# Issuing a transformer trunk's late stores from GpSimd's queue instead of SyncE's

## The chip, the core and the metric

The program runs on one NeuronCore of a Trainium2 chip. The core has a matmul engine (TensorE, "PE" in the profile; its weight loads are shown apart as "PEld"), a vector engine (VectorE, "DVE"), an engine for activation functions and copies (ScalarE, "ACT"), GpSimd ("POOL") and SyncE ("SP"), which computes nothing and here issues transfers. Each engine works through its own list of instructions in order; where an instruction needs a result of another engine or a transfer, it waits, and everything behind it on that engine waits too. Data moves between the chip's large memory (DRAM in the program) and the on-chip memory (SBUF) by DMA. A DMA is put in a queue by an engine's instruction and carried out by sixteen DMA engines; the profile names the queue fed by SP "hardware_dynamic" and the one fed by GpSimd "software_dynamic".

The metric is the device time of one execution in microseconds (us), as the median of several runs.

## The reference

Two streams of 512 tokens of width 1024 ("prompt", stream 0, and "sample", stream 1) go through the same two layers with the same weights, all in float32.

```python
def _trunk(x, ...):
    for i in range(DEPTH):                       # 2 layers
        xn = _rms_norm(x, pre_norm_g[i])
        if i % N_MIXERS == 0:
            h = _rwkv7_branch(xn, ...)           # layer 0: a scan over tokens, both directions
        else:
            h = _natten_branch(xn, ...)          # layer 1: neighbourhood attention
        x = x + _rms_norm(h, post_norm_g[i])
    return x

def _wkv7_scan(r, decay, k, v, a, b, reverse):   # layer 0, 16 heads of 64
    def step(s, inp):
        r_t, w_t, k_t, v_t, a_t, b_t = inp
        sa = jnp.einsum('bhvk,bhk->bhv', s, a_t)
        s = s * w_t[:, :, None, :] + sa[..., None] * b_t[:, :, None, :] + v_t[..., None] * k_t[:, :, None, :]
        return s, jnp.einsum('bhvk,bhk->bhv', s, r_t)
...
def _natten_branch(xn, w_in, b_in, rpb, w_o, b_o):
    proj = xn @ w_in + b_in                      # 1024 -> 4 x 1024
    q, k, v, z = jnp.split(proj, 4, axis=-1)
    o = _neighbourhood_attention(heads(q) * (HEAD_DIM ** -0.5), heads(k), heads(v), rpb)
    return (o.reshape(bsz, t, D_INNER) * jax.nn.silu(z)) @ w_o + b_o
```

Layer 0 also has projections r, k, v, z and an output projection `w_o`. In layer 1 each of the 512 tokens (a grid of 8 x 64) attends to an 8 x 16 window, with a learned bias per head.

## The kernel before

Activations lie transposed: 128 features on the partitions, 512 tokens along the row, so a 512 x 1024 matrix is eight tiles of 128 x 512 floats (256 KB each). One column of a projection is a sum over eight such tiles, and each float32 product is made of three matmuls (`gemm`, lines 428 to 430: high part of the weight by high and low part of the data, low part by high part). Weights come from DRAM as `raw` tiles (three buffers), and ACT (line 377) and DVE (line 378) split them into `whi` and `wlo`.

The program has three stages. First both streams are normalized and some projections made. Then the scan stage (`scan_phase`) runs the scans of both streams and, woven into them by an order written out by hand with an estimated clock, the projections of stream 1 and the beginning of layer 1 for stream 0. What follows is `rest`, the stage behind the scan, from about 1169 us on: the last two columns of stream 0's q, k, v, z (`inproj(0, ...)`), the output projection of stream 1's layer 0 (`out0(1)`), the attention of stream 0 (`heads(0, p)`, eight pairs of heads), its output projection and result (`out1(0)`), the projections of stream 1 in layer 1 (`inproj(1, ...)`) with the attention of stream 1 woven in (`heads(1, p)`), and `last`, which makes stream 1's output by tokens. `rest` is not ordered by hand: a scheduler that estimates times places the instructions of each engine, so a moved store also moves what stands around it.

A projected column doesn't go straight to its reader: `qkvz` computes the tile `o` (a `tmp` buffer of five) from PSUM (the matmul engine's output memory) on DVE (line 1393) and ACT (lines 1397 to 1407), and `save` (line 327) stores it to DRAM as `dq`, `dk`, `dv` or `dz`. `heads` later loads it back (`load`, line 333) as `q`, `k`, `v`, `z`, into buffers of its own; the load waits until the store has landed. From q and k PE makes scores (`sc`, line 1437), DVE adds the bias and takes the maximum (line 1448), ACT takes exponentials (line 1451), DVE scales (line 1453), PE transposes (`pt`, line 1455), ACT copies (`pts`, line 1458), PE multiplies by the values (`po`, line 1470), and DVE applies the gate z (line 1479).

Which queue a store goes to is decided in `store`, by the flag `away`:

```python
    def store(self, kind):
        return self.nc.gpsimd if self.away and kind not in ("y", "x1", "h") else self.nc.sync
```

`away` is set to True at the start of `scan_phase` (line 1646) and to False at the start of `rest` (line 1750). So within the scan stage most stores are issued by GpSimd, and in `rest` all by SP, whose list also holds all the loads: weights, biases, q, k, v, z and the residual tiles.

Of the kernel before, what the change touches and what calls it, by code (L numbers as in the profile page):

```python
# [19 lines left out]
P = 128  # L20
# [211 lines left out]
class Trunk:  # L232
# [1252 lines left out]
    def out1(self, s):  # L1485
        nc = self.nc
        x = self.os[s]
        acc = self.t("acc1", pool=self.ap)
        hs = []
        for p in range(NP):  # L1490
            ps = yield from self.gemm(self.weight(self.a["w_ao"][p]), x, self.OUT1[p % 4])
            h = self.t("oa", (P, T), NP, F32, self.ap)
            nc.scalar.activation(h, ps, AF.Identity, bias=self.vec("bo", p))
            self.sumsq(acc, h, p, nc.vector if p == NP - 1 else nc.vector)
            hs.append(h)
            yield
        yield from self.rstds(acc, lambda: self.mm)
        rstd = acc
        for k, h in enumerate(hs):
            x = self.load(self.t("xr", bufs=self.NXR), self.sp["x1", s, k])  # L1500
            one = nc.vector.scalar_tensor_tensor(h, h, self.vec("post1", k), rstd, op0=ALU.mult, op1=ALU.mult)
            self.behind(one, self.mq)
            (nc.vector if k % 2 else nc.vector).tensor_tensor(h, h, x, op=ALU.add)
            nc.sync.dma_start(self.a["y"][s][k * P:(k + 1) * P, :], h)
            yield

    def by_token(self):
# [211 lines left out]
    def run(self):  # L1719
        self.todo = [(s, pb) for s in range(2) for pb in range(4)]  # L1720
        self.made, self.hid, self.shift = set(), {}, {}
        self.did = Counter()
        self.xz, self.os = [], [[], []]
        self.spare = None
        self.away = False
        mid, prep, first = ExitStack(), ExitStack(), ExitStack()
        self.banks(mid, pf=1, pm=5 - self.SG - self.ZY, us=1)
        if self.SG:
            self.banks(mid, pg=self.SG)
        self.zs = ExitStack()  # L1730
        self.banks(self.zs, zy=self.ZY)
        self.gt = "zy"
        self.lp = self.pool(first, "right")
        a = self.prelude(0)
        for _ in range(self.FIRST):
            next(a)
        a = both(a, self.prelude(1))
        run(self.columns(0, "z", self.xz), (a, 1))
        run(self.columns(0, "k", self.shifted(0, 1)), (a, 1))
        run(a)  # L1740
        self.xr = self.shifted(0, 0)
        first.close()
        self.front = self.pool(mid, "right")
        self.pp = self.pool(prep, "right")
        self.AHEAD, self.AHEADW = self.SCAN_A, self.SCAN_W
        self.scan_phase(mid)
        self.rest(prep, mid)

    def rest(self, prep, mid):
        self.away = False  # L1750
        prep.close()
        mid.close()
        self.banks(self.stack, pg=self.PG, pt=self.PT, po=1, sc=1, pm=5 - self.PG - self.PT)
        self.gt = "pg"
        self.ap = self.pool(self.stack)
        queue = [self.heads(0, p) for p in range(self.NPA)]

        def attention():
            while True:
                if queue and next(queue[0], self) is self:  # L1760
                    queue.pop(0)
                    continue
                yield

        a = attention()
        for p in range(self.NPA, NP):
            run(self.inproj(0, self.xa, p), (a, self.POST0))
            queue.append(self.heads(0, p))
        run(self.out0(1), (a, self.POST))
        while queue:  # L1770
            next(a)
        o = self.out1(0)
        if self.HS:
            with self.tc.high_priority(self.HS):
                next(o)
        n = KT * NP
        for _ in self.norm0(1):
            for _ in range(min(n, 3)):
                next(o)
                n -= 1  # L1780
        for _ in range(n):
            next(o)
        x = self.x1
        xt = self.by_token()
        for p, cs in [(p, range(4)) for p in range(6)] + [(6, range(3)), (7, range(3)), (6, (3,)), (7, (3,))]:
            run(self.inproj(1, x, p, cs), (a, self.POST3), (o, self.POST2), (xt, self.POST4))
            if 0 in cs:
                queue.append(self.heads(1, p))
        run(o)
        while queue:  # L1790
            next(a)
        self.last()
# [125 lines left out]
```

## Time and profile before

| | us |
|---|---|
| median of 3 runs | 1663.77 (1659.5 to 1666.94) |
| the profiled execution's own time | 1661.37 |
| its span, first to last instruction | 1659.6 |
| PE busy in it | 1557.8 (94%) |
| DVE busy | 1226.3 (74%) |
| ACT busy | 984.7 (59%) |
| POOL busy | 145.4 (9%) |
| mean granted TensorE clock | 0.979 |

The profile is one execution recorded instruction by instruction. A row of its timeline gives the start, the duration, the engine (SPq is SP's issuing of DMAs), the line of the kernel, the operation, "out<-in" by the names of the tiles, how many rows were merged (x2), and in brackets the idle time just before on that engine and what ended it. A row of waits names the waiting engine and line, then the operation that it waited for, the total, how many times, and the longest. "DMA dk<-tmp" as a releaser is the landing of the transfer that stored `tmp` to `dk`. Matmuls overlap in the pipeline, so the step from one start to the next, rather than the duration, is what a matmul costs.

### The profile page before, as it was taken

The numbers are of one execution on the slowest core, as the hardware profiler recorded it, in microseconds if no ns is written. First come the engines' busy times: TensorE is split into PE (matmuls) and PEld (weight loads), VectorE is DVE, ScalarE is ACT, GpSimd is POOL, SyncE is SP. The second block draws the span as 40 slices with busy tenths as digits, with TensorE's granted clock in tenths as the row PEclk, the third lists the DMA queues.
The fourth block names the chain that finished last, engine by engine and source line by source line (L and its number), as shares of the span: only waits on it lengthen the run. The fifth ranks groups of instructions, "written<-read, shape, count | busy, mean of one in ns | idle before, by whom it ended". The sixth has DMA issues, their size and how long they took to land.

```text
span 1659.6 us, 46414 instructions
## 1 busy us (share of the span) xinstructions
PE 1557.8 (94%) x18826; PEld 1193.4 (72%) x18826; DVE 1226.3 (74%) x2725; ACT 984.7 (59%) x1979; POOL 145.4 (9%) x278
## 2 busy tenths in 40 slices
PE   7989888898989998999988999999999999999998
PEld 5867566776767776776766777777777788777776
DVE  8995669688789787897788897855676585754564
ACT  5443665766756677665575665454677665555562
POOL 0000113311101224010000011000000000000000
PEclk9989999999999999999987999999999999999999
DMA  6435678776676788675867675554864346655553
GB/s 212 160 126 173 206 243 280 221 244 214 228 255 225 222 260 247 219 255 173 253 220 228 196 253 165 182 189 129 289 219 156 102 153 229 214 159 172 165 159 108
DMA packets 179894, 336.27 MB, mean 203 GB/s; under 512 B 20928, under 2 KB 53824, under 8 KB 179680
## 3 DMA queue, kind: packets, MB, share of 16 engines
q1 hardware_dynamic: 160864, 268.28, 50.2%
q0 software_dynamic: 18816, 65.02, 11.9%
q8 instruction: 148, 2.42, 0.6%
q14 instruction: 66, 0.54, 0.1%
HBM read 227.71 MB, written 105.51 MB: 201 GB/s over the span
## 4 chain that ended last, share of the span: by engine, by line
PE 46%; DVE 7%; DMA 6%; ACT 5%; issue 3%; POOL 0%; SPq 0%; DVEq 0%; ACTq 0%; POOLq 0%
PE pg L428 6%; PE pg L429 5%; PE pg L430 5%; PE pm L811 4%; PE pm L812 3%; PE pm L813 3%; PE sc L1437 2%; PE pf L1099 2%; DMA dk<-tmp 2%; PE po L1470 2%; PE us L1218 1%; PE pt L1455 1%; PE zy L1171 1%; PE us L1198 1%; PE zy L1222 1%
## 5 line engine op out<-in xcount | busy, mean ns | idle before, releaser
L811 PE MATMUL pm<-act,whi 128*128 128x512 f32 x640 | 283.6, 443 | 11.9 <-ACT whi L730 5.0
L812 PE MATMUL pm<-act,whi 128*128 128x512 f32 x640 | 257.1, 402 | 10.6 <-DVE act L758 6.5
L813 PE MATMUL pm<-act,wlo 128*128 128x512 f32 x640 | 256.1, 400 | 6.0 <-DVE wlo L732 5.9
L811 PEld LDWEIGHTS pm<-act,whi 128*128 128x128 f32 x640 | 122.0, 191 | 55.3 <-issue 11.4
L377 ACT CAST whi<-raw 128x512 fp32r<-128x512 f32 x148 | 91.5, 618 | 114.0 <-PE pg L429 67.1
L428 PE MATMUL pg<-act,whi 128*128 128x512 f32 x384 | 157.9, 411 | 0.4 <-DVE tmp L1393 0.4
L430 PE MATMUL pg<-act,wlo 128*128 128x512 f32 x384 | 152.1, 396 | 0.0
L429 PE MATMUL pg<-act,whi 128*128 128x512 f32 x384 | 152.0, 396 | 0.0
L812 PEld LDWEIGHTS pm<-act,whi 128*128 128x128 f32 x640 | 122.5, 191 | 36.6 <-DVE act L758 15.8
L813 PEld LDWEIGHTS pm<-act,wlo 128*128 128x128 f32 x640 | 122.4, 191 | 36.2 <-DVE wlo L732 9.6
L378 DVE TENSOR_TENSOR wlo<-raw,whi 128x512 fp32r<-128x512 f32 x148 | 101.5, 687 | 54.6 <-ACT whi L377 52.6
L732 DVE TENSOR_TENSOR wlo<-raw,whi 128x512 fp32r<-128x512 f32 x160 | 109.0, 684 | 35.5 <-ACT whi L730 35.2
L730 ACT CAST whi<-raw 128x512 fp32r<-128x512 f32 x160 | 97.9, 618 | 44.6 <-PE pm L812 23.4
L428 PEld LDWEIGHTS pg<-act,whi 128*128 128x128 f32 x384 | 72.2, 188 | 15.8 <-issue 3.3
L430 PEld LDWEIGHTS pg<-act,wlo 128*128 128x128 f32 x384 | 72.2, 188 | 15.5 <-issue 0.7
L429 PEld LDWEIGHTS pg<-act,whi 128*128 128x128 f32 x384 | 72.4, 189 | 13.2 <-issue 1.5
L1003 DVE TENSOR_TENSOR etmp<-N 128x30 f32<-128x30 f32 (+14 forms) x240 | 78.6, 328 | 4.3
L1005 DVE TENSOR_TENSOR N<-etmp,N 128x30 f32<-128x30 f32 (+14 forms) x240 | 78.7, 328 | 4.0
L1448 DVE CUSTOM_DVE_ANT_0 sb<-sc,bias 128x256 f32<-128x256 f32 x128 | 49.3, 419 | 34.6 <-PE pt L1455 22.7
L1451 ACT ACTIVATE sb<-sb,mx 128x256 f32<-128x256 f32 x128 | 64.0, 503 | 8.6 <-DVE mx L1450 8.1
L1099 PE MATMUL pf<-cab 64*64 64x128 f32 (+1 forms) x2048 | 66.6, 266 | 0.8 <-issue 0.8
L1210 ACT COPY X<-us 64x256 f32<-64x256 f32 x128 | 46.9, 366 | 25.3 <-PE zy L1077 21.4
(401 smaller groups left out, 3603.0 us busy)
## 6 DMA issues: line engine op xcount, KB each, us to landing
dab<-ab POOLq DMA_DIRECT2D x32, 1024.0 KB, 7.0
cab<-dab SPq DMA_DIRECT2D x64, 512.0 KB
raw<-in_w_in_dram SPq DMA_DIRECT2D x128, 256.0 KB
bias<-in_rpb_dram SPq DMA_DIRECT2D x32, 384.0 KB
raw<-in_w_z_dram SPq DMA_DIRECT2D x32, 256.0 KB
raw<-in_w_k_dram SPq DMA_DIRECT2D x32, 256.0 KB
raw<-in_w_r_dram SPq DMA_DIRECT2D x32, 256.0 KB
k<-dk SPq DMA_DIRECT2D x32, 256.0 KB
```

Source lines behind the costliest of these rows:

```text
L377: self.nc.scalar.copy(hi, src)
L378: (eng or self.nc.vector).tensor_tensor(lo, src, hi.bitcast(F32), op=ALU.subtract)
L428: nc.tensor.matmul(ps, hi, x[k][0], start=(k == 0), stop=False)
L429: nc.tensor.matmul(ps, hi, x[k][1], start=False, stop=False)
L430: self.mm = nc.tensor.matmul(ps, lo, x[k][0], start=False, stop=(k == KT - 1))
L730: nc.scalar.copy(hi, raw[h])
L732: nc.vector.tensor_tensor(lo, raw.pop(h), hi.bitcast(F32), op=ALU.subtract)
L811: nc.tensor.matmul(ps, hi[:, at], xh, start=(k == 0), stop=False)
L812: nc.tensor.matmul(ps, hi[:, at], xl, start=False, stop=False)
L813: nc.tensor.matmul(ps, lo[:, at], xh, start=False, stop=(k == KT - 1))
L1005: vt.tensor_tensor(N[:, q + 1:, :q], tv, N[:, q + 1:, :q], op=ALU.add)
L1099: end = nc.tensor.matmul(st.f[half(a), h, 0, d, g] if st.last else st.f[half(a), h, :, d, g], ab[half(h), d, g, 2 * e[d] + 1 - a], rt if s ...
```

## The change

The line that sets `away` back to False at the start of `rest` is gone, so the stores that `save` makes there, other than those of kinds y, x1 and h, are issued by GpSimd: eight tiles q, k, v, z of stream 0 (two columns of each), 32 of stream 1, and eight `xt` tiles (rows of stream 1's layer-0 result on the way back to tokens). The eight result stores of stream 0 in `out1` are written out as GpSimd's too. That makes 56 stores of 256 KB. Stream 1's result rows, stored in `last`, stay on SP, as do all loads.

```diff
@@ out1
             self.behind(one, self.mq)
             (nc.vector if k % 2 else nc.vector).tensor_tensor(h, h, x, op=ALU.add)
-            nc.sync.dma_start(self.a["y"][s][k * P:(k + 1) * P, :], h)
+            nc.gpsimd.dma_start(self.a["y"][s][k * P:(k + 1) * P, :], h)
             yield
@@ rest
     def rest(self, prep, mid):
-        self.away = False
         prep.close()
         mid.close()
```

Up to the end of the scan stage the lists of all engines are the same. Behind it the scheduler orders them anew. Three places show how.

On SP, in stream 1's projections: the load of `k` for one pair of heads waits for the store of the same tile. Rows with + are new, rows with - are gone; `raw` are weights, `bias` the attention's bias.

```order
 L333 DMA raw_20409<-in_w_in_dram 128x512
-L327 DMA dq_3784_20175<-tmp_20172 128x512
+L333 DMA raw_20411<-in_w_in_dram 128x512
 L333 DMA q_3847_20431<-dq_3784_20175 128x512
-L333 DMA raw_20411<-in_w_in_dram 128x512
 L333 DMA bias_20739<-in_rpb_dram 128x768 x2
 L333 DMA raw_20497<-in_w_in_dram 128x512
-L327 DMA dk_3802_20257<-tmp_20254 128x512
 L333 DMA k_3848_20433<-dk_3802_20257 128x512
 L333 DMA raw_20499<-in_w_in_dram 128x512
```

The two stores leave the list; the loads that wait for them stay, and one weight load now stands ahead of the load of q.

On PE, at the scores that read this same `k` (`sc_20465`, four matmuls in the list), among the projection's matmuls:

```order
 L429 MATMUL pg_20370<-act_18625,whi_20366 128x512
 L430 MATMUL pg_20370<-act_18626,wlo_20367 128x512
-L1437 MATMUL sc_20465<-k_3848_20433,q_3847_20431 128x256
+L428 MATMUL pg_20370<-act_18645,whi_20366 128x512
 L1470 MATMUL po_20153<-pts_20338,vtok_20132 64x128 x4
 L1470 MATMUL po_20153<-pts_20305,vtok_20132 64x128 x4
-L1437 MATMUL sc_20465<-k_3848_20433,q_3847_20431 128x256 x3
-L428 MATMUL pg_20370<-act_18645,whi_20366 128x512
+L1437 MATMUL sc_20465<-k_3848_20433,q_3847_20431 128x256 x4
 L429 MATMUL pg_20370<-act_18644,whi_20366 128x512
```

The first of the four score matmuls moves back by one projection matmul and the whole run of `po`, so `k` is needed later. The same move is made for the other three score groups around which PE waits for `k` (`sc_19843`, `sc_20776`, `sc_21050`).

On PE, in stream 0's attention, early in `rest`: before, two groups of scores of one pair of heads stand close together.

```order
L1437 MATMUL sc_17325<-k_3067_17286,q_3066_17284 128x256 x4
L1455 MATMUL pt_17181<-cc,sb_17207 128x128
L1455 MATMUL pt_17224<-cc,sb_17225 128x128 x2
L1455 MATMUL pt_17224<-cc,sb_17240 128x128 x2
L430 MATMUL pg_17302<-act_12735,wlo_17299 128x512
L428 MATMUL pg_17302<-act_12913,whi_17298 128x512
L429 MATMUL pg_17302<-act_12912,whi_17298 128x512
L430 MATMUL pg_17302<-act_12913,wlo_17299 128x512
L1424 MATMUL pm_17584<-cc,v_3156_17578 128x128 x4
L1437 MATMUL sc_17470<-k_3067_17286,q_3066_17284 128x256 x4
L1470 MATMUL po_17094<-pts_17252,vtok_17058 64x128 x4
L1470 MATMUL po_17094<-pts_17219,vtok_17058 64x128 x4
```

After the change the rows ahead of the second group are these, and the first group stands 27 rows ahead of it instead of 9:

```order
L429 MATMUL pg_17302<-act_12602,whi_17298 128x512
L430 MATMUL pg_17302<-act_12603,wlo_17299 128x512
L1470 MATMUL po_17094<-pts_17252,vtok_17058 64x128 x4
L1470 MATMUL po_17094<-pts_17219,vtok_17058 64x128 x4
L1437 MATMUL sc_17470<-k_3067_17286,q_3066_17284 128x256 x4
L1455 MATMUL pt_17330<-cc,sb_17331 128x128 x2
L1455 MATMUL pt_17330<-cc,sb_17343 128x128 x2
```

The attention of this pair is spread over more projection matmuls. An earlier pair moves the other way: before, `sc_16935` stood behind a run of `po` as `sc_17470` does here now; after the change only these rows of PE lie between it and the group ahead of it.

```order
L1437 MATMUL sc_16844<-k_2952_16815,q_2951_16813 128x256 x4
L1455 MATMUL pt_16713<-cc,sb_16714 128x128 x2
L1455 MATMUL pt_16713<-cc,sb_16726 128x128 x2
L1455 MATMUL pt_16743<-cc,sb_16744 128x128 x2
L1424 MATMUL pm_17059<-cc,v_3010_17053 128x128 x4
L1455 MATMUL pt_16743<-cc,sb_16761 128x128 x2
L1437 MATMUL sc_16935<-k_2952_16815,q_2951_16813 128x256 x4
```

Here the two groups of scores have moved closer together.

## Prediction

> **What bounds the kernel now.** I read the page's busy times first, then busy time by stretches behind the scan, then the waits of PE and of SP's queue there, and last the timeline around the longest of these waits. The stretches (start and end in us, length, then busy us and instructions of PE, PEld, DVE, ACT, POOL, the granted clock, the DMA share, GB/s):
>
> ```profile
> 1169.00:1320.00 151.00, 147.66 (x957) 116.56 (x956) 101.31 (x393) 103.28 (x250) 0.00 (x0) 1.00 0.60 201
> 1320.00:1440.00 120.00, 118.08 (x629) 95.28 (x628) 81.55 (x198) 70.28 (x140) 0.00 (x0) 1.00 0.59 187
> 1440.00:1610.00 170.00, 167.95 (x939) 129.97 (x938) 98.51 (x323) 92.55 (x212) 0.00 (x0) 1.00 0.54 169
> 1610.00:1660.00 50.00, 41.91 (x207) 33.15 (x205) 24.25 (x49) 14.21 (x33) 0.00 (x0) 0.95 0.33 109
> ```
>
> All that changes lies in these 491 us. Up to 1610 us PE is busy for 433.7 of 441; the last 50 us end with a tail on other engines. POOL does nothing at all. So a transfer can win only what PE stands idle for, and PE's waits behind the scan are few (who waits, for whom, total us, times, longest):
>
> ```profile
> PE sc L1437 <- DMA k<-dk: 2.1, 4, 0.6
> PE sc L1437 <- DVE mx L1448: 1.5, 1, 1.5
> PE pm L470 <- DVE tmp L466: 1.1, 1, 1.1
> PE pg L428 <- ACT oa L1493: 0.8, 1, 0.8
> PE pt L1455 <- DVE sb L1453: 0.7, 1, 0.7
> PE po L1470 <- ACT pts L1458: 0.6, 2, 0.3
> PE pg L428 <- DVE tmp L1393: 0.4, 1, 0.4
> ```
>
> Together 7.2 us. The first row is the one that the stores touch directly. SP's queue, over the same stretch, waits much longer for stores to land, because the loads of q, k, v, z stand in it:
>
> ```profile
> SPq L333 <- DMA dk<-tmp: 32.7, 8, 6.8
> ...
> SPq L333 <- DMA dq<-tmp: 18.5, 8, 3.5
> SPq L333 <- DMA dz<-tmp: 17.3, 8, 2.8
> SPq L333 <- DMA dv<-tmp: 12.8, 6, 2.7
> ```
>
> Here 81 us of store landings look like the prize, but nearly all of them pass while PE works. The timeline at one pair of heads shows how much is left:
>
> ```profile
> 1494.20 0.90 SPq L333 DMA_DIRECT2D bias<-in_rpb_dram  x2
> 1495.21 0.36 SPq L333 DMA_DIRECT2D raw<-in_w_in_dram  x1
> 1495.67 0.38 SPq L327 DMA_DIRECT2D dk<-tmp  x1
> 1502.78 0.33 SPq L333 DMA_DIRECT2D k<-dk  x1
> ...
> 1505.39 0.70 PE L1437 MATMUL sc<-k,q 64*128 64x256 f32 x2 [0.48 <-DMA k<-dk]
> ```
>
> The store of k is issued at 1495.67 and its reader can be issued only at 1502.78, 7.11 us later; the load takes until 1505.39; and PE stands still for 0.48 us of these ten.
>
> **The change, part by part.**
>
> *The issuing.* SP loses 56 issues and POOL gains them. On SP one took 0.38 us above, so 21 us leave SP's list; on POOL a store of the same kind, in the scan stage, took 0.54, so POOL gets 30 us in 491 in which it has nothing to do:
>
> ```profile
> L327 POOL DMA_DIRECT2D dk<-tmp x14: 540/541/569, 358.4 to 1151.1; - x14
> ...
> DMA to landing us min/median/max: 2.3/3.5/8.2
> ```
>
> The issue is 0.16 us longer for each tile on its way. The stores to `dxt`, `dv` and the result rows cost nothing: no PE wait above has them as its cause. POOL now waits in its list for each tile in turn; behind a waiting store stand only other stores, and they stood in the same order behind each other on SP. What else moves past SP's 56 gaps are the weight loads, and no row of PE's waits names a weight.
>
> *The landing of k.* On SP's queue it took at most 7.11 us; on POOL's, beside a busier DMA system, 3.5 in the middle and 8.2 at worst. Two bias loads and a weight load go out just ahead of it on SP's queue, and a store in a queue of its own need not stand behind them. I take 3.5, which brings k 3.5 us earlier. By itself that ends the first row of PE's waits, and the new order does so a second time: ahead of the scores PE now has one projection matmul and a run of `po` (16 in the trace). What a projection matmul costs stands in the timeline:
>
> ```profile
> 1429.42 0.40 PE L430 MATMUL pg<-act,wlo 128*128 128x512 f32 x1
> 1429.65 0.38 PE L1455 MATMUL pt<-cc,sb 128*128 128x128 f32 x2
> 1429.79 0.47 PE L428 MATMUL pg<-act,whi 128*128 128x512 f32 x1
> ```
>
> What a run of `po` costs stands in the chain of waits (start, us, what):
>
> ```profile
> 1262.61 1.03 PE po L1470 x16
> ```
>
> The projection matmul takes 0.23 (from 1429.42 to the next start at 1429.65) and the run of `po` 1.03, so 1.26 us of work lie in front of a wait that was 0.6 at most. The term is -2.1 us; its ends are 0 and -2.1.
>
> *PE's work in the new order.* The matmuls are the same, but what their mixture costs changes. Two transposes put between projection matmuls delay the next by 0.14 (1429.65 to 1429.79); four in one run cost this:
>
> ```profile
> 1427.26 0.60 PE L1455 MATMUL pt<-cc,sb 128*128 128x128 f32 x4
> 1427.62 0.48 PE L430 MATMUL pg<-act,wlo 128*128 128x512 f32 x1
> ```
>
> That is 0.36, so breaking a run saves 0.08. Counted over the two lists of PE, transposes go over into a projection matmul at 79 places instead of 69: ten breaks, -0.8 us. Since runs of scores and values are broken and joined too, I give it the ends 0 and -1.6.
>
> *The stall around 1230 us.* This is the second row of PE's waits, with the fifth and the last:
>
> ```profile
> 1221.99 0.81 SPq L333 DMA_DIRECT2D bias<-in_rpb_dram  x2
> 1223.37 1.34 SPq L333 DMA_DIRECT2D xr<-dy  x2
> ...
> 1228.20 1.34 ACT L377 CAST act<-xr 128x512 fp32r<-128x512 f32 x2 [3.31 <-DMA xr<-dy]
> 1231.70 1.14 PE L1437 MATMUL sc<-k,q 64*128 64x256 f32 x8 [1.53 <-DVE mx L1448]
> 1234.54 1.13 PE L1455 MATMUL pt<-cc,sb 128*128 128x128 f32 x6 [0.68 <-DVE sb L1453]
> 1236.43 0.49 PE L428 MATMUL pg<-act,whi 128*128 128x512 f32 x1 [0.43 <-DVE tmp L1393]
> ```
>
> The loads of y come late behind a bias load that waits for its buffer; ACT stands 3.31 us, and after it PE three times, 2.64 us in all, each time for DVE. In the new list the scores that waited 1.53 (`sc_17470`) stand 27 rows behind the group before instead of 9, so their wait goes. The bias load stays where it blocks SP, so ACT's wait may stay and reach PE elsewhere. I take -1.5, nearest to the row that the order removes, with the ends 0 and -2.6.
>
> *A new wait.* `sc_16935` has moved close to the group ahead of it (12 transposes between, 12 times 0.07 to 0.09 by the two rows above, about 1 us), while DVE must first have read that group. No row of before shows so close a pair; the nearest is the 1.53 us at `sc_17470`, an estimate for the worst, and 0 for the best. DVE has no load to wait for here, so I take +0.5.
>
> *The end.* The last gate tile is the place where a slower store would hurt:
>
> ```profile
> 1615.04 0.34 SPq L327 DMA_DIRECT2D dz<-tmp  x1
> 1617.09 0.34 SPq L333 DMA_DIRECT2D z<-dz  x1
> ...
> 1619.96 0.69 DVE L1479 TENSOR_TENSOR tmp<-po,z 128x512 f32<-128x512 f32 x1 [2.58 <-DMA z<-dz]
> 1621.34 0.69 DVE L378 TENSOR_TENSOR os<-tmp,os 128x512 fp32r<-128x512 f32 x1 [0.69 <-ACT os L377]
> 1624.91 0.39 PE L1557 MATMUL pg<-act,os 128*128 128x512 f32 x1
> ```
>
> The store lands within 2.05 us, the product with z is ready at 1622.03 and PE takes it at 1624.91. A landing of 3.5 uses 1.5 of these 2.9 us: nothing, until POOL's landing passes 4.9.
>
> Sum: -2.1 - 0.8 - 1.5 + 0.5 = -3.9 us, with ends of -6.3 and +1.5. The profiled execution took 1661.37 (1.77 more than its span), so 1657.5 for its like; the median of the runs shown is 2.4 above it, 1663.77, and becomes 1659.9.
>
> **What the skill says against it.** POOL's issues took 540 to 569 ns while DVE was busy around them, and the landings had a middle of 3.5 us, so no row here shows POOL held up by DVE. The Trainium skill, SBUF — State Buffer, section "SBUF: two separate sides", says that GpSimd cannot write a transfer's descriptors while DVE runs an operation that takes the port they share, and gives about 620 ns alone against 3100 overlapped; by that figure, an estimate, every store would land 2.5 us later. The sum would then still be -3.9, since 3.5 and 2.5 are less than 7.1. The trace does not agree so far, in the scan stage; the stage behind it has no GpSimd row.
>
> The other side of the trace is that k's store takes 7.11 us behind three loads and z's 2.05 with none issued just ahead. The Trainium skill, DMA: Bandwidth & Descriptors, section "Issuing engines are not separate DMA queues", says that transfers of all issuers share sixteen engines and a second issuer saves only issuing time; by it the landing stays, and the -2.1 would rest on the new order alone.
>
> **The rivals.**
>
> 1. *The stalls stay where they are* (no change that counts). For it: SP's loads still wait for buffers, and ACT's 3.31 us come from a load, which stays on SP. Against it: the order puts 1.26 us ahead of k's wait. If only the mixture's -0.8 and the new wait's +0.5 remain, -0.3 and 1663.5.
> 2. *Late stores, slower than before.* If POOL's stores land late in this stage, k comes late at each pair of heads of stream 1. It decides from where the landing passes the old 7.11 by 0.66 (1.26 less the largest old wait of 0.6), less 0.16 for the longer issue: 7.6 us. Each us beyond costs one us at each of the eight pairs; +8.3 us net of the other terms' -1.8 needs 10.1 / 8 = 1.3 more, 8.9 us at every pair, against the longest seen among 14, 8.2. Time from 1672.
> 3. *The order waits, slower than before.* The attention of stream 0 has been moved forward against the projections. If each of its 16 score groups waited as the longest did, 1.53, it would cost 24 us, 1684; it decides at half of them. Against it: only one pair of groups was moved together.
> 4. *All of PE's waits go, and more.* 7.2 and 1.6 are 8.8 us: 1655.0. Against it: two of the waits (lines 470 and 428 behind ACT's line 1493) hang on sums that no store touches.
>
> **How the numbers follow.** A measurement of this kernel can tell about 0.5%, 8.3 us, from no change, so faster means under 1655.5 and slower over 1672.1. My forecast has 0.58 with a range of its own of 1657.5 to 1665.3; rival 1 has 0.22; rival 2 has 0.07, rival 3 0.06, rival 4 0.07. The runs of before spread over 7 us, which carries a few of the forecast's cases over the lower bound: faster 0.09, same 0.78, slower 0.13. The range for 8 in 10 is 1653 to 1670: the forecast's ends and half the runs' spread on either side, and a little of rivals 2 to 4.
>
> **What would show it.** Right: no or nearly no row of PE waiting for `k<-dk`; landings of POOL's `dk` near 3.5 us; the wait of SP for `dk` well below 32.7; PE busy for almost all of the stretch from 1169 to 1610, which ends 2 to 6 us earlier; the tail as long as before. Wrong: PE waits for k of a us and more, landings over 7.6 us, or many new waits of `sc`, `pt` or `po` for DVE and ACT between 1180 and 1290 us.

## The result and the profile after

Over 20 runs of each kernel the median went from 1663.44 us to 1658.20 us, a ratio of 0.9969 (95% interval 0.9956 to 0.9982). That is 0.31% less, within the 0.5% that the prediction called no change, and 1.7 us below the predicted 1659.9. The profiled execution of the changed kernel took 1657.03 us (span 1655.2), 4.34 less than that of before.

Busy time by stretches behind the scan in the changed kernel (columns as in the prediction):

```profile
1169.00:1320.00 151.00, 147.97 (x952) 116.00 (x952) 101.18 (x391) 102.37 (x250) 4.32 (x8) 1.00 0.61 199
1320.00:1440.00 120.00, 118.07 (x629) 95.38 (x628) 80.79 (x197) 70.17 (x140) 13.56 (x25) 1.00 0.59 193
1440.00:1610.00 170.00, 169.80 (x972) 132.47 (x971) 102.05 (x336) 96.37 (x219) 11.89 (x22) 1.00 0.54 168
1610.00:1656.00 46.00, 37.59 (x173) 29.68 (x171) 19.90 (x36) 10.24 (x25) 0.54 (x1) 0.94 0.32 107
```

POOL now issues 56 stores in 30.3 us, and the third stretch, stream 1's projections with its attention, has almost no idle PE: 0.20 us of 170 where it was 2.05. The waits of PE behind the scan:

```profile
PE po L1470 <- ACT pts L1458: 1.5, 1, 1.5
PE pm L470 <- DVE tmp L466: 1.1, 1, 1.1
PE pg L428 <- ACT oa L1493: 0.9, 1, 0.9
PE sc L1437 <- DVE mx L1448: 0.6, 1, 0.6
PE pt L1455 <- DVE sb L1453: 0.5, 1, 0.5
PE pg L428 <- DVE tmp L1393: 0.4, 1, 0.4
PE pm L1424 <- DMA v<-dv: 0.2, 1, 0.2
```

The row `k<-dk` (2.1) is gone, and a wait of 0.2 for `v` is new. The other six make 5.0 us, against 5.1 before: the 1.5 that scores waited for DVE is gone, and 1.5 of another kind is there. On SP's queue the waits for stores read now:

```profile
SPq L333 <- DMA dk<-tmp: 26.2, 8, 5.1
SPq L333 <- DMA dz<-tmp: 25.3, 8, 4.9
...
SPq L333 <- DMA dv<-tmp: 7.8, 7, 3.3
...
SPq L333 <- DMA dq<-tmp: 5.8, 6, 1.8
```

The wait for `dk` fell by 6.5, those for `dq` and `dv` by 12.7 and 5.0, and that for `dz` rose by 8.0; together they fell from 81 to 65 us. Such a wait begins only when SP comes to the load, so it isn't the time of a landing. From the issue of `k`'s store to the issue of its load, at the seven pairs of heads behind 1400 us, it took 3.9 to 5.4 us with a middle of 4.9, against 2.1 to 7.2 with a middle of 6.1 before. For `dk` on POOL's queue, behind the scan:

```profile
L327 POOL DMA_DIRECT2D dk<-tmp x10: 540/541/543, 1174.6 to 1577.2; - x10
...
DMA to landing us min/median/max: 3.0/5.0/6.2
```

The issue takes 541 ns, as in the scan stage, but the landing has a middle of 5.0 us and not 3.5.

To place the difference I cut both executions at starts of the same instructions. The cuts are in groups of instructions by line, whose rows give, between the durations and the shapes, the first and the last start. Before, then after: the scan's last matmul, the first and the last group of transposes that bring `xt` back to tokens, and the last matmuls of the program.

```profile
L1222 PE MATMUL zy<-X,R x1024: 222/222/270, 336.5 to 1146.0; 128*64 128x64 f32 x171
L1514 PE MATMUL pt<-cc,h x16: 270/272/273, 1364.0 to 1394.7; 128*128 128x128 f32 x16
L1514 PE MATMUL pt<-cc,hh x16: 270/272/273, 1368.8 to 1399.4; 128*128 128x128 f32 x16
L1559 PE MATMUL pm<-whi,os x4: 394/394/397, 1649.4 to 1651.5; 128*128 128x512 f32 x4
```

```profile
L1222 PE MATMUL zy<-X,R x1024: 222/222/270, 336.1 to 1145.0; 128*64 128x64 f32 x171
L1514 PE MATMUL pt<-cc,h x16: 270/272/273, 1363.8 to 1394.6; 128*128 128x128 f32 x16
L1514 PE MATMUL pt<-cc,hh x16: 270/272/273, 1368.6 to 1399.3; 128*128 128x128 f32 x16
L1559 PE MATMUL pm<-whi,os x4: 394/394/397, 1645.1 to 1647.2; 128*128 128x512 f32 x4
```

| stretch, us | before | after | difference |
|---|---|---|---|
| up to the scan's last matmul | 1146.0 | 1145.0 | -1.0 |
| early: to the first `xt` transposes | 217.9 | 218.8 | +0.9 |
| the `xt` transposes, first to last | 35.5 | 35.5 | 0.0 |
| late: to PE's last matmul | 252.1 | 247.9 | -4.2 |
| the rest of the execution | 9.9 | 9.8 | -0.1 |

(The last row is the execution's own time less the end of the row above, 1661.37 - 1651.5 and 1657.03 - 1647.2; the rows differ from 4.34 by rounding.) The lists of all engines are the same up to the scan's end, so the -1.0 there is scatter and no effect of the change. What the change did lies in the late stretch; the early one got a little longer.

Inside the late stretch it can be counted. Each pair of heads has one place where the scores of its first group stand among the matmuls of the projection. The time from the start of the last projection matmul ahead of them to the start of the first one behind them is the cost of that place. Without a wait, before (timeline of PE):

```profile
1474.50 0.39 PE L430 MATMUL pg<-act,wlo 128*128 128x512 f32 x1
1474.81 0.70 PE L1437 MATMUL sc<-k,q 64*128 64x256 f32 x2
1475.44 1.09 PE L1470 MATMUL po<-pts,vtok 128*64 128x128 f32 x16
1476.46 1.13 PE L1437 MATMUL sc<-k,q 64*128 64x256 f32 x6
1477.52 0.50 PE L428 MATMUL pg<-act,whi 128*128 128x512 f32 x1
```

and after:

```profile
1503.07 0.39 PE L428 MATMUL pg<-act,whi 128*128 128x512 f32 x1
1503.38 1.09 PE L1470 MATMUL po<-pts,vtok 128*64 128x128 f32 x16
1504.41 1.14 PE L1437 MATMUL sc<-k,q 64*128 64x256 f32 x8
1505.47 0.50 PE L429 MATMUL pg<-act,whi 128*128 128x512 f32 x1
```

The same 24 matmuls, with the projection matmul ahead of them, take 3.02 us where the run of scores is split in two and six around the run of `po`, and 2.40 where it is whole (3.03 and 2.41 unrounded). Nothing waits in either. So a place can cost more in two ways, and PE's waits show only one of them. The table gives the cost of each of the six places around which PE waited for `k` or the scores were split, and what of it is over the same kind of place without a wait:

| six places, us | before | after |
|---|---|---|
| split 4 and 4 | 3.27 (0.66 over), 2.61 | none |
| split 2 and 6 | 3.03, 3.57 (0.54 over), 3.41 (0.38), 3.74 (0.71) | 3.03 |
| whole | none | 2.41 (five times) |
| sum | 19.63 | 15.08 |

Of the 4.55 us, the waits are 0.66 + 0.54 + 0.38 + 0.71 = 2.29 (the row of PE's waits had 2.1) and the splits the other 2.26. The late stretch got 4.2 shorter, so these six places account for it to within 0.4 us.

### The profile page after: what moved, and what is told of

It is laid out like the page before. It is cut to its first block, busy times and chain, and to the rows that moved or that the text cites. A ratio compares the mean times of both kernels' runs of the same rounds, so it can differ in the third digit from the quotient of the medians.

```text
span 1655.2 us, 46478 instructions
## 1 busy us (share of the span) xinstructions
PE 1559.5 (94%) x18826; PEld 1197.2 (72%) x18826; DVE 1225.7 (74%) x2725; ACT 983.8 (59%) x1979; POOL 175.7 (11%) x334
## 4 chain that ended last, share of the span: by engine, by line
PE 49%; DVE 7%; ACT 5%; DMA 3%; issue 3%; POOL 0%; DVEq 0%; SPq 0%; ACTq 0%; POOLq 0%
PE pg L428 6%; PE pg L429 6%; PE pg L430 6%; PE pm L811 4%; PE pm L812 3%; PE pm L813 3%; PE sc L1437 2%; PE po L1470 2%; PE pf L1099 2%; PE pt L1455 2%; PE us L1218 1%; PE zy L1171 1%; PE us L1198 1%; PE zy L1222 1%; DVE ab L925 1%
```

## The experiments

Three theories stood against each other. *The queue*: stores land earlier from POOL, because on SP they stand behind bias and weight loads; the wait for `k` ends for that reason. *The order*: the scheduler put the scores behind one more projection matmul and the run of `po`, and that alone takes the time, whichever queue the stores use. *Scatter or something small*: the 5 us of the medians come from other stores, or from nothing. Each run was timed beside the kernel before on its own chip; the times compared are of that pair. Where a table below says "late", it is the late stretch defined above.

### Only stream 1's k on POOL's queue

```diff
@@ save (on the kernel before)
-        self.store(kind).dma_start(d, src)
+        (self.nc.gpsimd if kind == "k1" and s == 1 else self.store(kind)).dma_start(d, src)
```

> Of all the stores only the eight k tiles of stream 1 go to GpSimd; PE's list keeps four of the five split score runs (first score matmul ahead of the run of po). Queue theory (k lands sooner in a queue of its own, and that is what ends PE's waits): landing near 5 us as in the changed kernel against 7.1 on SP, PE's waits for k from 2.1 us to under 0.3, time about -2.1 us. Order theory (PE's waits end because its new order puts a projection matmul and a run of po ahead of the scores): the waits for k stay near 2 us and the time is that of the kernel before within 1 us.

The ratio was 1.0006 (0.9985 to 1.0027), and the late stretch 252.0 us, as before the change. The scheduler kept the scores split at five of the six places. One of them, in the timeline of this kernel:

```profile
1492.83 0.90 SPq L333 DMA_DIRECT2D bias<-in_rpb_dram  x2
1494.02 0.33 SPq L333 DMA_DIRECT2D raw<-in_w_in_dram  x1
1494.45 0.54 POOL L327 DMA_DIRECT2D dk<-tmp  x1 [29.49 <-ACT tmp L1399]
1502.88 0.33 SPq L333 DMA_DIRECT2D k<-dk  x1
...
1505.62 0.67 PE L1437 MATMUL sc<-k,q 64*128 64x256 f32 x2 [1.91 <-DMA k<-dk]
```

The store goes out on a queue of its own, and its reader is issued only 8.43 us later, 1.32 more than the 7.11 on SP's queue. With the same two bias loads and the same weight load issued ahead, a queue of its own brought the store no sooner to its end. This is the worst of the seven places: at five of them the store took 0.2 to 1.6 us longer than before to the issue of its load, at two 0.7 and 0.9 less, and at these two, still split, the waits of 0.34 and 0.64 were gone. PE's wait at the place shown grew from 0.48 to 1.91 us, by 1.43: here one us of later `k` is about one us of waiting. It is the only wait for `k` that is left, where there were four, and the total is nearly the same (1.9 against 2.1). The landings were 3.4 us at least, 6.3 in the middle, 8.4 at most. So the move of `k` by itself wins nothing.

### All of the change but stream 1's k

```diff
@@ save, and the result store of out1 on gpsimd (on the kernel before)
-        self.store(kind).dma_start(d, src)
+        (self.nc.gpsimd if kind in ("q1", "v1", "z1", "xt") or kind == "k1" and s == 0 else self.store(kind)).dma_start(d, src)
```

> All stores of the change but the eight k tiles of stream 1, which stay on SP; PE's list has the joined score runs as the changed kernel has. Queue theory: k still lands 6 to 7 us after its issue, PE waits for k as before (about 2 us), and the gain is about -2 us from the mixture alone. Order theory: the 1.26 us ahead of the scores hide a wait of at most 0.6, PE's waits for k go under 0.3, and the gain is the whole one, -4 to -5 us.

The ratio was 0.9992 (0.9970 to 1.0014): the time doesn't tell. The late stretch was 248.9 us and PE waited for no `k`, although `k`'s store had stayed on SP: in this order, too, the places where scores meet the projection cost 2.41, and one 2.61. That is 3.2 us less in the late stretch, short of the 4 to 5 expected, and the early stretch was 219.2, 1.3 longer than before. `k`, still on SP's queue, was there 4.8 us after its issue in the middle of the seven places, as soon as with the whole change (4.9) and sooner than alone on POOL's queue (6.3).

### The new order alone, all stores on SP

Here the scores of a pair's first group in stream 1 are held behind the run of `po` of the pair before, and nothing else is touched.

```diff
@@ heads (on the kernel before)
                         if last is not None:
                             self.behind(one, last)
+                        elif s == 1 and ns[0] == 0 and self.lastpo is not None:
+                            self.behind(one, self.lastpo)
                         last = one
@@ heads, after the loop that makes po
                             last = one
+                self.lastpo = last if s == 1 else None
```

> Every store stays on SP; only PE's order is changed, by holding the first scores of each pair of heads of stream 1 behind the last run of po of the pair before. No score run is split. Queue theory: k lands as late as before, 6 to 7 us, waits for k stay near 2 us, gain at most -2. Order theory: waits for k under 0.3 us, and -4 us in time: about -2.2 for the waits and -2 for the score runs that are no longer split.

The ratio was 0.9976 (0.9955 to 0.9997), and the late stretch 247.6 us, as short as with the whole change, which leaves one of the seven runs split where the hold leaves none. The same kernel was run once more, on another chip, together with one that is told in the next section:

> The kernel with all stores on SP and only the hold on PE's order, a second time, beside the one with GpSimd's stores. Order theory: late stretch 247.6 us again, the time about 4 us under the kernel before in the mean. Queue theory: PE's waits for k of 2 us or more appear in this execution.

The ratio was 0.9952 (0.9936 to 0.9969), late 247.2. Cuts of this run:

```profile
L1517 PE MATMUL pt<-cc,hh x16: 270/272/273, 1369.7 to 1400.4; 128*128 128x128 f32 x16
L1562 PE MATMUL pm<-whi,os x4: 394/394/397, 1645.6 to 1647.7; 128*128 128x512 f32 x4
```

All the stores lie on SP, and SP's queue waits as long for `k` as before the change (32.7):

```profile
SPq L333 <- DMA dk<-tmp: 32.3, 8, 6.2
```

PE, though, waits for no `k` at all in this run. An order with whole runs gives the whole gain without the queue.

### Only stream 1's q, k, v and z on POOL's queue, and the same with the hold

```diff
@@ save (on the kernel before)
-        self.store(kind).dma_start(d, src)
+        (self.nc.gpsimd if kind in ("q1", "k1", "v1", "z1") and s == 1 else self.store(kind)).dma_start(d, src)
```

> Only the 32 stores of q, k, v, z of stream 1 go to GpSimd; the early stage (stream 0's attention, 1169 to 1316 us) keeps the order of the kernel before. Both theories: the whole gain of the changed kernel, -4 to -5 us, since it lies behind 1400 us. If the early stage's new order or the xt and result stores had a part in it, this run would fall short of the changed kernel by more than 1 us.

The ratio was 0.9996 (0.9978 to 1.0014), the late stretch 248.1 and the early one 217.7. The late gain is there, yet the time doesn't show it: by the stretches 4.2 us (0.9975) were due, and the interval ends just short of that. By the measure set beforehand, the time, the early order or the other stores would have had a part in the gain. One reason to go by the stretches stands in the cuts of the profiled executions of this kernel and of the hold's first run:

```profile
L1222 PE MATMUL zy<-X,R x1024: 222/222/271, 338.5 to 1152.3; 128*64 128x64 f32 x171
```

```profile
L1222 PE MATMUL zy<-X,R x1024: 222/222/271, 333.8 to 1140.1; 128*64 128x64 f32 x171
```

PE's order up to this matmul is the same in both kernels, and in the kernel before, where it ended at 1146.0. Among all the profiled executions with this order it ended between 1140.1 and 1152.3 us: from one execution to another the scan stage scatters by nearly three times what the change is worth. This is why I go by stretches, and take the whole time only where several runs agree. One profiled execution can't say, though, whether the scan stage of this kernel is longer in the mean of its 12 executions. Their mean granted clock was 0.974, that of the kernel before beside them 0.976; whether that is the reason isn't shown. What makes the scan's end scatter wasn't found.

The same stores on POOL's queue, with the hold of the section before added:

> Stream 1's 32 stores of q, k, v, z on GpSimd and PE held so that no score run of stream 1 is split; early stage as before. With e11 (the same hold, all stores on SP) PE's two orders are nearly the same, so the pair shows the queue by itself. Order theory: late stretch 247 to 248 us in both, within 0.5 of each other, no PE wait for k in either. Queue theory: this one shorter by 1 us or more.

The ratio was 0.9953 (0.9935 to 0.9971) and the late stretch 246.9, against 247.2 and 0.9952 for the hold with every store on SP, on the same chip. The cuts of this run:

```profile
L1517 PE MATMUL pt<-cc,hh x16: 270/272/273, 1366.1 to 1396.7; 128*128 128x128 f32 x16
L1562 PE MATMUL pm<-whi,os x4: 393/394/397, 1641.5 to 1643.6; 128*128 128x512 f32 x4
```

PE waits for no `k` here either. `k` was there 5.1 us after its issue in the middle of the seven places, against 6.2 with the stores on SP, but there was no wait left for that to shorten. With the order nearly fixed, the queue is worth 0.3 us in the late stretch, which is within what two runs of one kernel differ by (247.6 and 247.2), and nothing in the time.

### Only stream 0's stores on POOL's queue

```diff
@@ save (on the kernel before)
-        self.store(kind).dma_start(d, src)
+        (self.nc.gpsimd if kind in ("q1", "k1", "v1", "z1") and s == 0 else self.store(kind)).dma_start(d, src)
```

> Only the eight stores of stream 0's q, k, v, z go to GpSimd; PE's order is new in the early stage and that of before in the late one. Both theories: late stretch 252 us with PE's waits for k of about 2 us, as before. Early stretch (scan's end to the first xt transpose) 218.5 to 219.5 against 217.9: the stall around 1230 us is gone and other waits of the same total have come, so nothing is gained there.

One execution: 1663.77 us beside 1661.15 for the kernel before. The early stretch was 218.6 and the late one 253.6, where the scores stayed split and PE waited for `k` three times (3.1 us, 1.6 at the longest). So stream 0's eight stores show no gain, and the waits for `k` scatter by a us between two kernels whose late places are split alike.

### Stream 1's bias loads out of the way of k

```diff
@@ heads (on the kernel before)
-            self.load(bias[:, h].rearrange("p a b -> p (a b)"), self.a["rpb"][2 * p + h])
+            (nc.gpsimd if s == 1 else nc.sync).dma_start(bias[:, h].rearrange("p a b -> p (a b)"), self.a["rpb"][2 * p + h])
```

> Stores as before on SP; only the bias loads of stream 1's attention (two of 384 KB just ahead of k's store) go to GpSimd's queue. If k's store lands late on SP because it stands behind those loads in the queue, the time from its issue to the issue of k's load falls from 6 to 7 us to under 5. If it lands late because the sixteen DMA engines share all queues' work, it stays at 6 us or more. PE keeps the split score runs, so the late stretch is 250 to 252 us.

One execution: 1660.07 us beside 1662.60 for the kernel before. Timeline at the pair of heads that was looked at before:

```profile
1494.81 0.42 SPq L327 DMA_DIRECT2D dk<-tmp  x1
1499.98 0.33 SPq L333 DMA_DIRECT2D k<-dk  x1
...
1504.05 0.70 PE L1437 MATMUL sc<-k,q 64*128 64x256 f32 x2
```

With the bias loads on POOL's queue (here issued 2.9 us ahead of it, where they stood 1.5 ahead), `k`'s store on SP's queue lands within 5.17 us instead of 7.11, and the scores wait for nothing. That lies between the bounds set beforehand (under 5, or 6 and more), so it doesn't tell whether the store stands behind those loads in the queue or shares the DMA engines with them. But the runs of scores stay split (the x2 in the last row): the six places cost 2.61, four times 3.03 and 2.61. The late stretch is 250.9 us, 1.2 less than before. This separates the two effects: to end the waits gives at most the 2.29 us that they held, here about half of it (0.7 came back as new waits for DVE and ACT), and the rest of the 4.2 needs the runs whole.

### Making k late

Two kernels were to find how late `k` may come before PE waits in the new order. One puts three stores of a constant tile in POOL's list ahead of each of stream 1's stores of `k`, the other four more stores of `k`'s own tile.

```diff
@@ save (on the kernel after; the first, then the second)
+        if kind == "k1" and s == 1:
+            ...
+            for j in range(3):
+                self.nc.gpsimd.dma_start(self.junk[j], self.cc)
```

```diff
+            for j in range(4):
+                self.nc.gpsimd.dma_start(self.junk[j], src)
```

> The changed kernel with three extra stores of 515 KB (a constant tile into unused DRAM) issued on GpSimd ahead of each k store of stream 1, so k lands later. If lateness over the break-even of 7.6 us costs PE one us for each us, with landings of k (its own issue to landing) of 9 to 11 us plus the extra issuing time of 1.6 us, PE waits for k 2 to 5 us at each of five or more pairs, 10 to 25 us in all. If the loads have more slack than that, the waits stay under 3 us in all.

> The changed kernel with four extra stores of the same k tile into unused DRAM ahead of the real one, on GpSimd. The real store is issued 2.2 us later and lands behind 1 MB. The scheduler knows of them and moves the first scores back by some 3 to 28 projection matmuls (0.7 to 6.4 us). Order theory: what decides is where the scores stand, so PE's waits for k stay under 2 us in all and the late stretch within 3 us of the changed kernel's 247.9, though k's load is issued 6 us or more after PE's last projection matmul of k. Late-store rival: 1 us lost for each us of landing over 7.6, 10 us or more.

Neither did what it was made for. In the first, the scheduler issued the extra stores in the program's first stage, since their data were ready, which gave PE another order there too; `k` landed in 3.9 to 6.6 us, and the late stretch was 248.3 (1667.05 us in all beside 1661.15, with the scan's end at 1153.5). In the second the landings got longer only by a little, to 5.9 us in the middle and 7.4 at most, from 4.9 and 5.4. No PE wait for `k` appeared, and the late stretch was 248.5 (1662.75 in all beside 1662.60). The scheduler had moved the scores back behind more projection matmuls at the same time, so this is no clean test either. What a landing beyond 7.6 us costs in the new order, the price of the prediction's rival 2, wasn't tested.

### The hold at every group, in both streams

```diff
@@ heads (on the kernel after; and the same on the kernel before)
+                        elif self.lastpo is not None:
+                            self.behind(one, self.lastpo)
...
+                self.lastpo = last
```

> The changed kernel, with every first score group of a pair of heads, of both streams, held behind the run of po before it, so that no score run is split any more. Order theory: the one split left in stream 1 (0.62 us more than an unsplit group) goes, and the three in stream 0's attention; the stretch from the last xt transposes to PE's end is 247 us or a little less (the changed kernel: 247.9; before: 252.1), and the early stretch falls by about 1 us if no new waits come. Queue theory: as the changed kernel.

> The same hold, but all stores on SP as in the kernel before. Order theory: the late stretch is the same as with the hold and GpSimd's stores, 247 us within 0.7, so the queue is worth nothing by itself. Queue theory: PE waits for k and the late stretch stays 2 us or more longer than with GpSimd's stores.

This was meant to keep every run of scores whole. It cost 65 us instead: 1.0381 (1.0354 to 1.0407) on the kernel after, 1.0386 (1.0361 to 1.0411) on the kernel before. (The profiled execution of the first took 5082 us where its five others took 1723 to 1732; why is not known.) In the second, PE's waits behind the scan show the start of it:

```profile
PE pt L1457 <- DVE mx L1454: 20.6, 8, 4.1
PE po L1472 <- ACT pts L1460: 11.5, 17, 1.5
```

Without the condition on the group, a pair's second group of scores also stands behind the pair's own first run of `po`, which needs the first group's softmax on DVE and ACT. PE then waits through it, up to 4.1 us a time. All its waits there make 44.8 us, 37.6 more than before, and that is not the whole loss. The granted clock was 0.92 from 1150 to 1330 us and 0.89 from 1330 to 1480, where the kernel before had 1.00 in both, and the score matmuls between 1200 and 1300 us took 517 ns in the mean instead of 404. From the clock alone that is 0.08 x 180 + 0.11 x 150 = 31 us, an estimate of the most that it cost. That the waits brought the clock down is not tested; PE's order is another one too. Whole runs are worth 0.6 us each only where the scores can be moved without standing in front of their own consumers.

### The kernels beside each other

| kernel | early | late | ratio (95%) |
|---|---|---|---|
| before | 217.9 | 252.1 | |
| after | 218.8 | 247.9 | 0.9969 (0.9956 to 0.9982) |
| stream 1's k on POOL | 217.9 | 252.0 | 1.0006 (0.9985 to 1.0027) |
| all but stream 1's k on POOL | 219.2 | 248.9 | 0.9992 (0.9970 to 1.0014) |
| stream 1's stores on POOL | 217.7 | 248.1 | 0.9996 (0.9978 to 1.0014) |
| hold, stores on SP | 218.5 | 247.6 | 0.9976 (0.9955 to 0.9997) |
| hold, stores on SP, again | 217.6 | 247.2 | 0.9952 (0.9936 to 0.9969) |
| hold, stream 1's stores on POOL | 219.0 | 246.9 | 0.9953 (0.9935 to 0.9971) |
| bias loads on POOL | 218.3 | 250.9 | one execution |
| stream 0's stores on POOL | 218.6 | 253.6 | one execution |

The late stretch falls into two sets, 250.9 to 253.6 where most runs of scores are split and 246.9 to 248.9 where they are whole, and the queue of `k`'s store doesn't sort them. The lowest ratios are 0.9952 and 0.9953, of the hold without and with stores on POOL, timed side by side; the hold's other timing gave 0.9976, and all three intervals overlap that of the change.

## Why the prediction was right, and where its steps were not

The time, the sign and the size were right. Several of the steps were not, and they cancelled; that the sum came out so near is in part luck.

**The issuing.** As predicted: 56 stores cost POOL 30.3 us of issuing, 0.54 us each, in a time in which it had nothing else to do. `dxt` and the result rows have no row among PE's waits; `dv` has one of 0.2 us.

**The landing of k (-2.1).** The size was right (the waits that ended hold 2.29), and of its two reasons the first was wrong as it was put. The prediction held that a store in a queue of its own need not stand behind the loads just ahead, and took 3.5 us for the landing; after the change it was 5.0 in the middle. It also read 7.11 as the longest on SP's queue; at the pair of 1556 us it was 7.22. `k` did come sooner than before (4.9 against 6.1 in the middle), but not by its own queue: alone on POOL's it took 6.3, and on SP's, with the other stores on POOL's, 4.8. The second reason, 1.26 us of work put in front of the scores, is enough by itself: the hold with every store on SP has no wait for `k`, though `k` is as late there as before. So is a landing near 5 us: with the bias loads moved and PE's old order no wait is left either. The change has both, and no run tells which of them ended its waits. That each us of landing is a us lost is borne out at the one place looked at in the old order (1.32 later, 1.43 more wait).

The Trainium skill, DMA: Bandwidth & Descriptors, section "Issuing engines are not separate DMA queues", says that a second issuer saves only issuing time. By that rule the queue itself had nothing to give here, and the times agree: 246.9 and 247.2 us in the late stretch with and without it. The landing did change with the loads ahead: 7.11 us, and 5.17 with the bias loads moved.

**PE's work in the new order (-0.8, ends 0 and -1.6).** This is the step whose reason failed. The prediction counted runs of transposes that are broken up by projection matmuls, and priced a break at a gain of 0.08 us. What counted were the runs of scores, 64 rows deep, split around a run of `po`: 0.62 us for a split of two and six, 0.20 for four and four. In the late stretch five places became whole, which gives 4 x 0.62 + 0.20 = 2.68, and the sixth became a split of two and six, 0.42 worse: -2.3 in all. In the early stretch the same price went the other way, as the next part shows, and outside of its waits PE lost 1.1 us there; another 0.2 was lost in the rest of the late stretch (beside the new wait of 0.2 for `v`). -2.3 + 1.1 + 0.2 is -1.0, close to the term, but by luck: nothing in the runs shows the ten broken runs of transposes. The prediction mentioned the runs of scores and gave them only a wider end; in the trace of before the five rows at 1474.50 would have shown it, had they been set beside a place where the run is whole.

**The stall around 1230 us (-1.5) and the new wait (+0.5).** Each of the two came out within its ends, and a third thing, which no step had, undid them. These are all of PE's waits between 1175 and 1300 us after the change (timeline):

```profile
1189.79 1.09 PE L1470 MATMUL po<-pts,vtok 128*64 128x128 f32 x16 [1.55 <-ACT pts L1458]
1194.49 1.13 PE L1437 MATMUL sc<-k,q 64*128 64x256 f32 x8 [0.60 <-DVE mx L1448]
1198.38 0.50 PE L428 MATMUL pg<-act,whi 128*128 128x512 f32 x1 [0.37 <-DVE tmp L1393]
1241.24 0.63 PE L1455 MATMUL pt<-cc,sb 128*128 128x128 f32 x4 [0.51 <-DVE sb L1453]
```

The cluster of 2.64 us around 1230 is gone, all of it, which is the end of the range of that term. The scores at 1194.49 are `sc_16935`, moved close to the group ahead; they wait 0.60, where 0.5 was taken. But the run of `po` at 1189.79 now waits 1.55 us for ACT, where two runs of `po` waited 0.29 each before, and ACT had been waiting itself. Before, then after (timeline of ACT, the cast of a weight tile ahead of the copies that `po` needs):

```profile
1187.07 0.62 ACT L377 CAST whi<-raw 128x512 fp32r<-128x512 f32 x1 [0.59 <-DMA raw<-in_w_in_dram]
```

```profile
1188.15 0.62 ACT L377 CAST whi<-raw 128x512 fp32r<-128x512 f32 x1 [1.58 <-DMA raw<-in_w_in_dram]
...
1188.68 1.06 ACT L1458 COPY pts<-pt 128x512 f32<-128x512 f32 x2
```

ACT stood 1.58 us for the weight instead of 0.59, and right behind that cast in ACT's list stood the copies for `po`. The prediction dismissed the weight loads because no row of PE's waits names a weight; the wait for one is named after ACT there. In sum the waits of this window went from 3.22 (0.29 + 0.29 and the 2.64) to 3.03 us, so -0.2 where -1.0 was forecast. The early stretch got 0.9 longer all the same, so about 1.1 us is in busy time. There the runs of scores that are split went from one (four and four) to three (two of them two and six). The trace after the change has their price: the place at 1257.6 and the one at 1275.6, both split, cost 3.88 us each, and the one at 1221.5, with the same 32 matmuls and the run whole, 3.25. Twice 0.63 is 1.26, which accounts for it; no run tried that stretch without the splits. Kernels with this early order had 218.6 to 220.2 us, those with the old one 217.6 to 219.0.

**The end.** The last gate tile cost nothing, as predicted:

```profile
1610.30 0.54 POOL L327 DMA_DIRECT2D dz<-tmp  x1 [12.08 <-DVE tmp L1407]
1612.61 0.34 SPq L333 DMA_DIRECT2D z<-dz  x1
```

It landed within 2.31 us (2.05 before), and from PE's last matmul on the two kernels are alike to 0.1 us.

**The sum.** -2.1 - 0.8 - 1.5 + 0.5 = -3.9 was forecast. By the same stretches it is -2.3 (waits for `k`) - 2.3 (split runs) + 0.4 (the rest of the late stretch) + 0.9 (early), which makes -3.3; the profiled executions differ by 4.3, of which 1.0 lies in the scan stage and is scatter. The medians differ by 5.2; -3.3 lies within the interval of the ratio (-3.0 to -7.3), and where the other 1.9 of the medians lies is not known.

**The rivals.** Rival 1 (the stalls stay) came true in the early stage only, and there by a new stall of the old size. Rival 2 (late stores) was nearer than its chance said: landings reached 6.2 against the 7.6 from where it decides, and 8.4 with `k` alone. What a landing beyond 7.6 costs in the new order stays open. Rival 3 did not happen; one pair of groups waited for its own order, not sixteen. Rival 4 did not either: 5.2 us of waits are left.

## What to carry to other kernels

Where a scheduler orders the instructions, a change of a transfer's queue is also a change of the order, so the order has to be priced, and tested apart from the queue: hold an order like the new one on the old queue, and one run tells most of it. On an engine that is busy for 99% of a stretch, waits can be only half of what an order costs, as here in the late stretch; the other half was in busy time, so compare the same instructions, joined and split, from start to start. And where an earlier stage scatters by more than the effect, cut the trace at equal instructions and compare the stretch that was changed.

## What the runs showed of the hardware that was not expected

- Breaking a run of eight score matmuls (64 rows deep, 64x256) around a run of `po` costs PE 0.62 us if it is broken in two and six, and 0.20 in four and four, with nothing waiting.
- A queue of its own didn't bring `k`'s store to its end sooner. From its issue to that of its load, in the middle of seven places, it took 6.1 us with all stores on SP's queue, 6.3 with `k` alone on POOL's, 4.8 with all but `k` on POOL's, and 4.9 with all of them there.
- POOL's issue took 540 to 543 ns for most of the 56 stores and 612 at most, while DVE was busy for 60 to 67% of the three long stretches. The Trainium skill, SBUF — State Buffer, section "SBUF: two separate sides", says that GpSimd cannot write descriptors while DVE holds the port that they share; no run here showed POOL held up in that way.
- The end of the scan stage lay between 1140.1 and 1152.3 us in kernels with the same order of PE up to there. Why is open; the mean granted clock alone doesn't sort them (0.978 and 0.974 in these two executions, but 0.974 also in the changed kernel's, which ended the stage at 1145.0).
- In the kernel with the hold at every group, PE stood idle 44.8 us behind the scan instead of 7.2, in waits of up to 4.1 us, and the granted clock there fell to 0.92 and 0.89 in two stretches where it had been 1.00. The waits and the clock together come near the 65 us lost (37.6 and at most 31).
